# Forgetting attention: in the first and third pair of query blocks, both blocks' last keys in one PSUM bank with one causal mask of 256 columns

## The chip, the cores and the metric

The kernel runs on one core of a Trainium2 chip. The metric is the time of one execution on the device, in microseconds (us), of the slowest core; here that is the only core. Five engines work beside each other and wait for one another through semaphores: PE (TensorE, matmuls and transposes), DVE (VectorE), ACT (ScalarE), POOL (GpSimd) and SP (SyncE, which issues the transfers). Matmul results go to PSUM, which the kernel uses as eight banks of 512 fp32 columns by 128 partitions.

## The reference, cut to what matters

The reference is a two-layer trunk over 1024 tokens of width 1024. Layer 0 mixes tokens with "forgetting attention" (16 heads of 64), layer 1 with gated linear attention; each is followed by a SwiGLU channel mixer. Only the attention is touched by the change. For every head and every block of 128 queries it computes this over the keys up to the block's end:

```python
for blk in range(S // Q_BLOCK):
    qs, qe = blk * Q_BLOCK, (blk + 1) * Q_BLOCK
    logits = jnp.einsum('bqhd,bkhd->bhqk', q[:, qs:qe], k[:, :qe]).astype(jnp.float32) * scale
    logits = logits + cum[:, :, qs:qe, None] - cum[:, :, None, :qe]
    mask = (qs + jnp.arange(Q_BLOCK))[:, None] >= jnp.arange(qe)[None, :]
    logits = jnp.where(mask[None, None], logits, -jnp.inf)
    p = jax.nn.softmax(logits, axis=-1).astype(v.dtype)
    outs.append(jnp.einsum('bhqk,bkhd->bqhd', p, v[:, :qe]))
```

The causal mask only bites in the last 128 keys of a block, where the queries stand against themselves.

## The kernel before, in words

**Units.** The eight blocks of 128 queries are taken in four pairs, g = 0 to 3; pair g holds the blocks 2g and 2g+1, whose keys are (2g+1)·128 and (2g+2)·128 wide. Heads go in pairs too: p = 0 to 7, a = 0 or 1. So there are 8·2·4 = 64 units (p, a, g), and within one head the pairs of blocks are taken in the order 0, 3, 1, 2 (ORDER, L1342). "First pair" below is g = 0 (128 and 256 keys), "third pair" is g = 2 (640 and 768 keys). There are 16 units of each.

**Scores (scores, L1259 to L1292).** For each of the two blocks (qi) the keys are cut into pieces of at most 512 columns (L1274). A piece gets a PSUM bank from the ring sr, which has two banks (L831). PE writes the piece with two matmuls, one with K1 (L1279) and one with KL, the low-order part of the keys (L1280). Both run 128 query columns as stationary operand, so each is preceded by a load of weights. The last piece of a block ends with a third matmul: the identity times a constant mask of 128 columns, both bf16, adds 1e30 above the diagonal (L1282). The scores are held with the sign turned, so a softmax subtracts the minimum. DVE then adds the cumulated forget gates to the piece, writes it to the SBUF tile lp and takes the running minimum along the row (L1285, two records each: the pass itself and the reading of its accumulator). When both pieces of a block are through, ACT takes the exponential with that minimum as bias and sums the row (L1289, again two records), DVE takes the reciprocal (L1290) and POOL scales the row (L1291).

**Outputs (outputs, L1294).** PE transposes the scaled rows in 128x128 blocks (trans, L1311), up to four to a bank of the ring tr (three banks); ACT and DVE split each into a high and a low part (L174, L175); then PE multiplies with the values (pv, L1323 and L1325). Outputs of a unit are emitted after the scores of the next unit (attention, L1354), so a third pair is transposed after the scores of the next head's first pair.

**The order.** Scores and outputs are generators; each yield gives a cost. weave (L130, called at L1386) takes turns between the attention of head pair p and the projections of head pair p+1 (matmuls of 512 and 256 columns, L305 to L307), in proportion to the costs yielded against the two totals 23.0 and 31.0. The attention of a p yields more than the 23.0 it is weighed by, so the projections run out first and the last part of every p has none beside it. A planner then orders each engine's instructions with an estimate of every duration; the order is fixed when the kernel is built, and LAGS (L1343) keeps a projection from running more than 18 attention steps ahead on PE. After the last p, the output projection and the channel mixer follow (from L1452).

Of the kernel before, what the change touches and what calls it, by code (L numbers as in the profile page):

```python
# [9 lines left out]
F32 = mybir.dt.float32  # L10
# [3 lines left out]
AF = mybir.ActivationFunctionType  # L14
ALU = mybir.AluOpType

P = 128
# [3 lines left out]
HALF = 512  # L21
# [32 lines left out]
def trunk(ctx, tc, x, c, ada_w, ada_b, norm1_g, norm2_g, ffn_w_in, ffn_w_out,  # L54
          fox_w_in, fox_b_f, fox_w_out, gla_w_in, gla_w_a2, gla_b_a, gla_g_o,
          gla_w_out, final_g, out, dbg=None, stop=None):
    nc = tc.nc
# [9 lines left out]
    def ps_rings(*counts):  # L67
        r, i = [], 0
        for n in counts:
            r.append(Ring(psp, [f"b{j}" for j in range(i, i + n)]))  # L70
            i += n
        assert i <= 8
        return r
# [35 lines left out]
    def psl(t, n=1):  # L109
        return slice(t * P, (t + n) * P)  # L110
# [49 lines left out]
    identb = cst.tile([P, P], BF16, name="identb")  # L160
# [9 lines left out]
    maskb = cst.tile([P, P], BF16, name="maskb")  # L170
# [265 lines left out]
    def last_of(e):  # L436
        return next(i for i in reversed(nc.cur_bb.bb.instructions) if i.engine == ENG[e])
# [393 lines left out]
    sr, tr, orr, pj = ps_rings(2, 3, 1, 2)  # L831
# [427 lines left out]
    def scores(u):  # L1259

        p, a, g = u
        t = qkt[p]
        Qs, K1, KL = (t["QA"], t["KA"], t["KLA"]) if a == 0 else (t["QB"], t["KB"], t["KLB"])
        cm = cums[2 * p + a]
        if g < 2:
            both = lpr([P, (4 * g + 3) * P], F32, f"lp{p}{a}{g}")
            lps = [both[:, 0:(2 * g + 1) * P], both[:, (2 * g + 1) * P:]]
        else:
            lps = [lpr([P, (2 * g + 1 + i) * P], F32, f"lp{p}{a}{g}{i}") for i in range(2)]
        st = sm.tile([P, 2, 4], F32, tag="st", bufs=4, name=f"st{p}{a}{g}")  # L1270
        for qi in range(2):
            qb = 2 * g + qi
            qs, lp, Wd, mcur = psl(qb), lps[qi], (qb + 1) * P, 3e38
            cuts = (0, 384, 640) if Wd == 640 else (0, Wd) if Wd <= HALF else (0, HALF, Wd)  # L1274
            for n_, (k0, k1) in enumerate(zip(cuts, cuts[1:])):
                ps = sr([P, k1 - k0], F32, f"s{p}{a}{qb}{k0}")
                early = u == (0, 0, 0)
                diag = k1 == Wd
                nc.tensor.matmul(ps, Qs[:, qs], K1[:, k0:k1], start=True, stop=False)  # L1279
                nc.tensor.matmul(ps, Qs[:, qs], KL[:, k0:k1], start=False, stop=not diag)  # L1280
                if diag:
                    nc.tensor.matmul(ps[:, k1 - k0 - P:], identb, maskb, start=False, stop=True)  # L1282
                mnew = st[:, qi, n_:n_ + 1]
                with tc.issue_after(v_last) if early else ExitStack():
                    nc.vector.tensor_tensor_reduce(lp[:, k0:k1], ps, cm[:, k0:k1], 1.0, mcur,  # L1285
                                                   ALU.add, ALU.min, mnew)
                mcur = mnew
                yield max(0.22, 0.00085 * (k1 - k0))
            nc.scalar.activation(lp, lp, AF.Exp, bias=mcur, scale=-1.0, accum_out=st[:, qi, 2:3])  # L1289
            nc.vector.reciprocal(st[:, qi, 3:4], st[:, qi, 2:3])  # L1290
            nc.gpsimd.tensor_scalar(lp, lp, st[:, qi, 3:4], 1.0, op0=ALU.mult, op1=ALU.mult)  # L1291
        return lps  # L1292

    def outputs(u, lps):  # L1294
# [59 lines left out]
    def attention(p):  # L1354
        for a in range(2):
            for g in ORDER:
                u = (p, a, g)
                lps = yield from scores(u)
                if p:
                    ada0p(0.8)  # L1360
                if pending[0] is not None:
                    yield from finish(*pending[0])
                pending[0] = (u, lps)
        if p == 7:
            yield from finish(*pending[0])
# [15 lines left out]
    v_last = last_of("D")  # L1381
# [95 lines left out]
    early = [s_ for s_ in rest if s_ in list(vring.q) + qk_all + list(cumr.q)]  # L1477
# [1042 lines left out]
```

## Time and profile before

| what | us |
|---|---|
| median of 3 timed runs | 2358.49 |
| lowest and highest of them | 2356.21 and 2358.67 |
| the profiled execution's own time | 2358.25 |
| its span, first to last instruction | 2356.5 |
| attention on PE, first to last start of its matmuls | 95.3 to 601.8 |

The profile is of one execution. Its span leaves out 1.75 us around the instructions (2358.25 - 2356.5). Records give the start of an instruction and how long it took; of matmuls, which are pipelined, the distance from one start to the next is the better measure of what one costs.

### The profile page before, as it was taken

Reading aid. Unit: us, or ns where it says so; the run is one execution under the profiler, and the core shown is the slowest. Engines: PE = TensorE matmul, PEld = TensorE weight load, DVE = VectorE, ACT = ScalarE, POOL = GpSimd, SP = SyncE. Lnnn points to the kernel's source line nnn. Section 1 sums busy time; section 2 is a strip of 40 time slices with the busy share of each in tenths; the row PEclk is TensorE's granted clock in tenths of the full one; section 3 lists DMA queues with packets and bytes.
Section 4 is the critical chain, followed back from the end, with each engine's and each line's share of the span. In section 5 each row is a group of like instructions: output and inputs, shape, how many; then the busy total and the mean of one; then the engine's idle time right before and its main releaser. Section 6 shows DMA issues by size and latency. Waiting matters only on the chain. (4 is left out here: it accounts for less than half of the span.)

```text
span 2356.5 us, 35548 instructions
## 1 busy us (share of the span) xinstructions
PE 2327.9 (99%) x12168; PEld 1980.9 (84%) x12168; DVE 1778.1 (75%) x2957; ACT 1122.5 (48%) x2166; POOL 1126.3 (48%) x995
## 2 busy tenths in 40 slices
PE   8999999999999999999999999999999999999999
PEld 7888888888888888888878898898888888888878
DVE  6578787886788888886787665678787777876776
ACT  6656655665443333345234644344453333345235
POOL 1334544533445666664643431345446665665631
PEclk8999999999999999999999999999999999999999
DMA  8423333332435545458674442554435444458574
GB/s 266 144 90 106 102 121 95 121 129 96 143 101 167 187 161 173 160 192 298 224 272 158 138 134 87 146 182 166 145 111 164 165 150 155 148 204 298 199 277 136
DMA packets 349614, 383.38 MB, mean 163 GB/s; under 512 B 25372, under 2 KB 286648, under 8 KB 349432
## 3 DMA queue, kind: packets, MB, share of 16 engines
q1 hardware_dynamic: 349432, 381.11, 49.1%
q8 instruction: 96, 1.57, 0.3%
q14 instruction: 86, 0.70, 0.1%
HBM read 279.76 MB, written 101.25 MB: 162 GB/s over the span
## 5 line engine op out<-in xcount | busy, mean ns | idle before, releaser
L174 ACT CAST o_s<-xv_s 128x512 fp32r<-128x512 f32 (+1 forms) x392 | 236.5, 610 | 343.0 <-PE p_b L307 250.0
L175 DVE TENSOR_TENSOR o_s<-xv_s,o_s 128x512 fp32r<-128x512 f32 (+1 forms) x392 | 331.9, 851 | 44.8 <-ACT o_s L174 44.0
L307 PE MATMUL p_b<-B,o_s 128*128 128x512 f32 x608 | 236.0, 389 | 0.0
L306 PE MATMUL p_b<-B,o_s 128*128 128x512 f32 x608 | 235.9, 389 | 0.0
L305 PE MATMUL p_b<-B,o_s 128*128 128x512 f32 x608 | 235.4, 390 | 0.0
L938 POOL TENSOR_TENSOR ex_s<-xv_s,xv_s 128x512 f32<-128x512 f32 (+1 forms) x64 | 96.2, 1503 | 259.0 <-DMA xv_s<-in_ffn_w_in_dram 119.9
L1291 POOL TENSOR_SCALAR lp_s<-lp_s,st 128x128 f32<-128x128 f32 (+7 forms) x128 | 98.0, 769 | 246.3 <-DVE st L1290 231.1
L305 PE MATMUL p_b<-T,o_s 128*128 128x512 f32 x480 | 186.8, 389 | 0.0
L306 PE MATMUL p_b<-T,o_s 128*128 128x512 f32 x480 | 186.7, 389 | 0.0
L307 PE MATMUL p_b<-T,o_s 128*128 128x512 f32 x480 | 181.1, 389 | 0.0
L307 PEld LDWEIGHTS p_b<-B,o_s 128*128 128x128 f32 x608 | 114.1, 188 | 23.8
L305 PEld LDWEIGHTS p_b<-B,o_s 128*128 128x128 f32 x608 | 114.2, 188 | 23.7 <-DVE x L1657 0.2
L306 PEld LDWEIGHTS p_b<-B,o_s 128*128 128x128 f32 x608 | 114.2, 188 | 23.5
L1289 ACT ACTIVATE lp_s<-lp_s,st 128x128 f32<-128x128 f32 (+7 forms) x128 | 99.3, 776 | 58.0 <-DVE st L1285 56.7
L940 POOL TENSOR_TENSOR xv_s<-ex_s,xv_s 128x512 f32<-128x512 f32 (+1 forms) x64 | 94.4, 1475 | 59.5 <-DVE o_s L175 56.5
L1657 DVE TENSOR_TENSOR ex_s<-ex_s,p_b 128x512 f32<-128x512 f32 x140 | 94.3, 682 | 37.4 <-PE p_b L307 37.3
L174 ACT CAST pt_s<-t_b 128x512 fp32r<-128x512 f32 (+1 forms) x160 | 79.7, 547 | 72.9 <-PE t_b L1311 72.3
L950 POOL TENSOR_TENSOR xv_s<-xv_s,xv_s 128x512 f32<-128x512 f32 x48 | 65.2, 1358 | 96.3 <-issue 52.3
L175 DVE TENSOR_TENSOR pt_s<-t_b,pt_s 128x512 fp32r<-128x512 f32 (+1 forms) x160 | 96.3, 630 | 15.9 <-ACT pt_s L174 15.4
L246 POOL TENSOR_TENSOR w_l_s<-w__s,w_h_s 128x256 fp32r<-128x256 f32 x90 | 69.4, 799 | 76.6 <-ACT w_h_s L242 58.8
L307 PEld LDWEIGHTS p_b<-T,o_s 128*128 128x128 f32 x480 | 90.1, 188 | 18.7
L306 PEld LDWEIGHTS p_b<-T,o_s 128*128 128x128 f32 x480 | 90.1, 188 | 18.6
(1532 smaller groups left out, 7396.8 us busy)
## 6 DMA issues: line engine op xcount, KB each, us to landing
xv_s<-in_ffn_w_in_dram SPq DMA_DIRECT2D x176, 256.0 KB, 3.2
hid_B<-x SPq DMA_DIRECT2D x66, 512.0 KB, 2.8
ad_s<-in_ada_w_dram SPq DMA_DIRECT2D x384, 64.0 KB, 2.3
hid_T<-x SPq DMA_DIRECT2D x44, 512.0 KB, 2.9
xv_s<-in_ffn_w_out_dram SPq DMA_DIRECT2D x88, 256.0 KB, 3.2
ada_s<-in_ada_w_dram SPq DMA_DIRECT2D x96, 128.0 KB, 2.8
T2o<-hid_T SPq DMA_DIRECT2D x22, 512.0 KB, 7.6
T1o<-hid_T SPq DMA_DIRECT2D x22, 512.0 KB, 8.6
```

Source lines behind the costliest of these rows:

```text
L174: nc.scalar.copy(hi, src)
L175: nc.vector.tensor_sub(lo, src, hi.bitcast(F32))
L246: (nc.gpsimd if i < 3 else nc.vector).tensor_sub(lo[:, cs], rw[:, cs], hi[:, cs].bitcast(F32))
L305: nc.tensor.matmul(ps, ah, bh, start=start, stop=False, skip_group_check=chain)
L306: nc.tensor.matmul(ps, ah, bl, start=False, stop=False, skip_group_check=chain)
L307: nc.tensor.matmul(ps, al, bh, start=False, stop=stop, skip_group_check=chain)
L938: nc.gpsimd.tensor_add(s1, a21, a22)
L940: nc.gpsimd.tensor_sub(a11, s1, a11)
L950: nc.gpsimd.tensor_sub(r[A12], r[A12], r[A11])
L1289: nc.scalar.activation(lp, lp, AF.Exp, bias=mcur, scale=-1.0, accum_out=st[:, qi, 2:3])
L1291: nc.gpsimd.tensor_scalar(lp, lp, st[:, qi, 3:4], 1.0, op0=ALU.mult, op1=ALU.mult)
L1657: nc.vector.tensor_add(d, d if src is None else dest(G, src), ps)
```

## The change

In the first and the third pair (g = 0 and g = 2) the last 128 or 256 keys of the two blocks are put side by side into one bank. For g = 0 that is 128 columns of the first block and 256 of the second; for g = 2 it is 256 of each, after a piece of 384 and one of 512 columns in banks of their own. PE writes all four score matmuls of the shared bank, then one matmul of the identity with the mask read twice (256 columns), which lands on the last 128 columns of each block. Only the first matmul of the bank carries the start flag. Then DVE takes the two parts, and each block's exponential, reciprocal and scaling follow its own part. The widths of the DVE passes, the exponentials and the scalings are the same as before. The number of pieces per bank, the places of the yields and the yielded cost of the first pair (0.22 in place of twice 0.22) are not. The second and the fourth pair (g = 1 and g = 3) keep their cuts and a mask for each block.

```diff
-            cuts = (0, 384, 640) if Wd == 640 else (0, Wd) if Wd <= HALF else (0, HALF, Wd)
-            for n_, (k0, k1) in enumerate(zip(cuts, cuts[1:])):
-                ps = sr([P, k1 - k0], F32, f"s{p}{a}{qb}{k0}")
...
+        least = [[], []]
+
+        def pair(o_, qi, k0, k1, start, stop):
+            qs = psl(2 * g + qi)
+            nc.tensor.matmul(o_, Qs[:, qs], K1[:, k0:k1], start=start, stop=False, skip_group_check=not stop)
+            nc.tensor.matmul(o_, Qs[:, qs], KL[:, k0:k1], start=False, stop=stop, skip_group_check=not stop)
+
+        def low(o_, qi, k0, k1):
+            got = least[qi]
+            mnew = st[:, qi, len(got):len(got) + 1]
+            with tc.issue_after(v_last) if u == (0, 0, 0) else ExitStack():
+                nc.vector.tensor_tensor_reduce(lps[qi][:, k0:k1], o_, cm[:, k0:k1], 1.0, got[-1] if got else 3e38,
+                                               ALU.add, ALU.min, mnew)
+            got.append(mnew)
+
+        def exps(qi):
+            lp = lps[qi]
+            nc.scalar.activation(lp, lp, AF.Exp, bias=least[qi][-1], scale=-1.0, accum_out=st[:, qi, 2:3])
             nc.vector.reciprocal(st[:, qi, 3:4], st[:, qi, 2:3])
             nc.gpsimd.tensor_scalar(lp, lp, st[:, qi, 3:4], 1.0, op0=ALU.mult, op1=ALU.mult)
+
+        W_ = [(2 * g + 1 + qi) * P for qi in range(2)]
+        if g in (0, 2):
+            cut = [0, 0] if g == 0 else [384, HALF]
+            for qi in range(2):
+                if g:
+                    ps = sr([P, cut[qi]], F32, f"s{p}{a}{g}{qi}")
+                    pair(ps, qi, 0, cut[qi], True, True)
+                    low(ps, qi, 0, cut[qi])
+                    yield 0.00085 * cut[qi]
+            n0 = W_[0] - cut[0]
+            ps = sr([P, n0 + 256], F32, f"s{p}{a}{g}")
+            pair(ps[:, 0:n0], 0, cut[0], W_[0], True, False)
+            pair(ps[:, n0:n0 + 256], 1, cut[1], W_[1], False, False)
+            m_ = ps.rearrange("p (a b) -> p a b", b=P)[:, n0 // P - 1::2]
+            nc.tensor.matmul(m_, identb, maskb.unsqueeze(1).to_broadcast([P, 2, P]), start=False, stop=True,
+                             skip_group_check=True)
+            for qi, c0, c1 in ((0, 0, n0), (1, n0, n0 + 256)):
+                low(ps[:, c0:c1], qi, cut[qi], W_[qi])
+                exps(qi)
+            yield 0.22 if g == 0 else 0.44
+            return lps
```

More of the change, by code (lines that the diff above doesn't have):

```diff
@@ L1270, in scores @@
         st = sm.tile([P, 2, 4], F32, tag="st", bufs=4, name=f"st{p}{a}{g}")
-        for qi in range(2):
-            qb = 2 * g + qi
-            qs, lp, Wd, mcur = psl(qb), lps[qi], (qb + 1) * P, 3e38
-            cuts = (0, 384, 640) if Wd == 640 else (0, Wd) if Wd <= HALF else (0, HALF, Wd)
-            for n_, (k0, k1) in enumerate(zip(cuts, cuts[1:])):
-                ps = sr([P, k1 - k0], F32, f"s{p}{a}{qb}{k0}")
[L1277 to L1289, printed above, removed]
@@ new lines, in scores @@
+        for qi in range(2):
+            cuts = (0, W_[qi]) if W_[qi] <= HALF else (0, HALF, W_[qi])
+            for k0, k1 in zip(cuts, cuts[1:]):
+                ps = sr([P, k1 - k0], F32, f"s{p}{a}{g}{qi}{k0}")
+                diag = k1 == W_[qi]
+                pair(ps, qi, k0, k1, True, not diag)
+                if diag:
+                    nc.tensor.matmul(ps[:, k1 - k0 - P:], identb, maskb, start=False, stop=True,
+                                     skip_group_check=True)
+                low(ps, qi, k0, k1)
+                yield max(0.22, 0.00085 * (k1 - k0))
+            exps(qi)
```

## The prediction, made before the changed kernel was run

> **What bounds the kernel now.** I read the page first (span, busy times, slices), then the stretch of the attention alone, then its waits on PE, then the order of time at a few places.
>
> ```profile
> span 2356.5 us, 35548 instructions
> PE 2327.9 (99%) x12168; PEld 1980.9 (84%) x12168; DVE 1778.1 (75%) x2957; ACT 1122.5 (48%) x2166; POOL 1126.3 (48%) x995
> PEclk8999999999999999999999999999999999999999
> ...
> 95.00:602.00 507.00, 501.52 (x3216) 439.15 (x3216) 378.69 (x960) 303.35 (x646) 221.36 (x316) 1.00 0.33 105
> ```
>
> PE has a record open for 99% of the span at a clock that is granted in full after the first slice. The last row is the attention by itself (us: length, busy PE, PEld, DVE, ACT, POOL; then clock and DMA): PE is open for 501.52 of 507.00 us, DVE for 378.69. PE therefore sets the pace here. From 602 us on, the page's slices show PE at 9 tenths to the end, so I let a microsecond of PE saved in the attention move everything behind it by a microsecond. The page's chain of work that ended last doesn't help: it covers 30% of the span and begins behind the attention.
>
> The waits on PE between 90 and 600 us (us in total, times, longest) are small:
>
> ```profile
> PE t_b L1311 <- POOL lp_s L1291: 2.8, 3, 1.9
> PE qk_b L305 <- DVE QB L860: 1.1, 2, 0.5
> PE s_b L1279 <- DVE st L1285: 0.4, 2, 0.3
> ```
>
> Transposes waiting for POOL's scaled rows are the largest; the wait for a score bank, which the change touches, is 0.4 us.
>
> **The change part by part.** *The masks.* A matmul's record is longer than what it costs, so I take start-to-start distances. In the order of time on PE (start, length, engine, line):
>
> ```profile
> 304.01 0.28 PE L1280 MATMUL s_b<-KLA,QA 128*128 128x256 f32 x1
> 304.14 0.23 PE L1282 MATMUL s_b<-maskb,identb 128*128 128x128 bf16 x1
> 304.18 0.36 PE L307 MATMUL vps_b<-wv_4h_s,h0l 128*128 128x256 f32 x1
> 304.38 0.28 PE L305 MATMUL vps_b<-wv_0h_s,h0h 128*128 128x256 f32 x1
> 304.49 0.28 PE L306 MATMUL vps_b<-wv_0l_s,h0h 128*128 128x256 f32 x1
> 304.61 0.28 PE L307 MATMUL vps_b<-wv_0h_s,h0l 128*128 128x256 f32 x1
> ...
> 349.17 0.28 PE L1280 MATMUL s_b<-KLA,QA 128*128 128x256 f32 x1
> 349.30 0.23 PE L1282 MATMUL s_b<-maskb,identb 128*128 128x128 bf16 x1
> 349.33 0.47 PE L305 MATMUL qk_b<-h0h,w_h_s 128*128 128x512 f32 x1
> 349.65 0.39 PE L306 MATMUL qk_b<-h0l,w_h_s 128*128 128x512 f32 x1
> 349.88 0.40 PE L307 MATMUL qk_b<-h0h,w_l_s 128*128 128x512 f32 x1
> ```
>
> A 256-column matmul in a steady row takes 0.12 us (304.49 to 304.61), a 512-column one 0.23 (349.65 to 349.88). Around the first mask, from L1280's start to the start after the next matmul, 304.38 - 304.01 = 0.37; two 256-column steps would be 0.24, so the mask costs 0.13. Around the second, 349.65 - 349.17 = 0.48 against 0.12 + 0.23 = 0.35: 0.13 again. The mask's own step is only 0.04; the rest is that the matmul behind it is stretched from 0.12 to 0.20, or from 0.23 to 0.32.
>
> ```profile
> L1282 PE MATMUL s_b<-maskb,identb x128: 229/230/233, 95.5 to 586.8; 128*128 128x128 bf16 x128
> ```
>
> There are 128 masks (8 blocks by 16 heads). The change turns two into one in 32 units (16 heads, two pairs each), so 96 stay, 32 of them 256 wide. What does a mask of 256 columns cost? The trace shows none. From below: a 256-column matmul with a weight load of its own steps at 0.12, so it may cost no more than the 128-column mask did. From above: 256 more columns cost 0.23 - 0.12 = 0.11, so 128 more could add 0.055. The stretch of the matmul behind the mask speaks for the low end: it says that the 128 columns are too short to cover the next weight load, so 128 more fill time that is lost today. I take 0.13 for it, as for a narrow one. Saved: 32 x 0.13 = **4.2 us**; with the upper price 32 x (0.13 - 0.055) = 2.4, with 0.12 for the wide mask 4.5.
>
> A rule of the Trainium skill speaks against this. "TensorE: Matmul & The Clock Gate", section "Back-to-back issue gap", gives an isolated matmul its columns over 2.4 GHz plus 2.5 ns; by that, one mask of 256 columns saves 2.5 ns against two of 128, and 32 of them 0.1 us. The same section says that this undercounts small matmuls where each has a weight load, and the 0.13 us above agrees with that.
>
> *What stays.* Score matmuls, DVE passes, exponentials and scalings keep their number and widths; no transfer is added, and SP's queue has nothing moved past it. One weight load per removed mask goes too; it is inside the 0.13.
>
> *The bank.* Four pieces of a third pair become three, two of a first pair one, so a shared bank is held until two DVE passes are through. The ring has two banks and the next score piece behind a shared bank takes the other one. PE's waits for a score bank are 0.4 us in all; between nothing and twice that, I take no change.
>
> *The later exponential.* This is the cost. In the third pair the first block's last part now stands in the shared bank, behind the 512-column piece of the second block and ahead of its last part. At the end of one p, on DVE (L1285), ACT (L1289) and POOL (L1291):
>
> ```profile
> 344.02 0.48 DVE L1285 CUSTOM_DVE_ANT_0 lp_s<-s_b,cum_s,st 128x256 f32<-128x256 f32 x1
> 344.61 0.83 ACT L1289 ACTIVATE lp_s<-lp_s,st 128x640 f32<-128x640 f32 x1 [0.55 <-DVE st L1285]
> 345.34 0.19 ACT L1289 ACTIVATION_READ_ACCUMULATOR lp_s<-lp_s,st 128x1 f32 x1
> 348.04 0.48 DVE L1285 CUSTOM_DVE_ANT_0 lp_s<-s_b,cum_s,st 128x256 f32<-128x256 f32 x1
> 348.45 0.08 DVE L1285 DVE_READ_ACCUMULATOR2_ANT st<- 128x1 f32 x1
> 348.93 0.94 ACT L1289 ACTIVATE lp_s<-lp_s,st 128x768 f32<-128x768 f32 x1
> 351.49 0.91 POOL L1291 TENSOR_SCALAR lp_s<-lp_s,st 128x768 f32<-128x768 f32 x1 [4.79 <-DVE st L1290]
> ```
>
> Before, the first block's minimum (344.02) and exponential (344.61) are done some 4 us ahead of the second's. After, the two minima are taken one behind the other: 0.48 + 0.08 = 0.56 us in front of the second's on DVE, and the first's exponential, 0.83 + 0.19 = 1.02, directly in front of the second's on ACT. It begins 0.56 before the second minimum is there, so the second exponential starts 1.02 - 0.56 = 0.46 after it. In all the second block's scaled rows come 0.56 + 0.46 = **1.0 us later**, the first block's some 4 us.
>
> Who waits for that? Behind a waiting transpose stands all of PE's queue. In the middle of a p there is room, at its end there is none:
>
> ```profile
> 316.30 0.91 POOL L1291 TENSOR_SCALAR lp_s<-lp_s,st 128x768 f32<-128x768 f32 x1 [0.46 <-DVE st L1290]
> 320.87 1.03 PE L1311 MATMUL t_b<-ident,lp_s 128*128 128x128 f32 x8
> ...
> 352.23 0.23 PE L1282 MATMUL s_b<-maskb,identb 128*128 128x128 bf16 x1
> 352.45 1.09 PE L1311 MATMUL t_b<-ident,lp_s 128*128 128x128 f32 x8
> 353.30 0.48 PE L305 MATMUL qk_b<-h0h,w_h_s 128*128 128x512 f32 x1
> ```
>
> In the first case POOL ends at 317.21 and PE transposes at 320.87, 3.7 us later. In the second it ends at 351.49 + 0.91 = 352.40 and PE starts at 352.45; the mask before stepped 0.22 rather than 0.04, so PE stood for some 0.2. Behind those transposes lie projections (353.30) that the planner can put ahead of them: it knows of the later exponential and fills with steps of 0.23, so what is left is about half such a step, 0.12, at the seven ends with a next p, less where POOL is early: I take 0.12 at six, **0.7 us**. Without that cover it is the first rival.
>
> *The sum.* 2358.25 (the profiled execution) - 4.2 + 0.7 = 2354.75, that is 3.5 less. The median of the runs is 2358.49, 0.24 above the profiled one; 3.5 below it is **2355.0 us**.
>
> **The rivals.** *A, slower: the late third pair stalls PE.* The planner's order holds a transpose at the ends of a p that the real exponential doesn't meet. Seen today once in full:
>
> ```profile
> 410.88 0.95 POOL L1291 TENSOR_SCALAR lp_s<-lp_s,st 128x640 f32<-128x640 f32 x1 [8.95 <-DVE st L1290]
> 411.88 0.55 PE L1311 MATMUL t_b<-ident,lp_s 128*128 128x128 f32 x3 [1.88 <-POOL lp_s L1291]
> ```
>
> PE stood 1.88 us there for the first block's rows. The price is 1.0 to 1.6 us an end (1.6 where the whole first exponential stands in front, 0.56 + 1.02), seven ends: 7 to 11, and 3 to 7 after the 4.2: middle 2358.49 + 4.8 = 2363.3. It cancels the gain from 0.6 an end (4.2 / 7). For it: no cover at the ends. Against it: work to put there, and only 2.8 us of such waits today. "Perfetto Trace Analysis", section "Matmuls", of the Trainium skill points the same way, asking that independent groups rotate through banks so that emptying one overlaps the next; the 0.4 us above is all that the trace shows of such a wait.
>
> *B, a smaller gain: the wide mask pays for its columns.* Saved 2.4 rather than 4.2, less 0.7: 2356.8. By the page's isolated rule it would be 2358.49 - 0.1 + 0.7 = 2359.1.
>
> *C, a larger gain: the new order also loses today's waits.* The 1.88 above, the rest of the 2.8 and the 0.4 go: 4.2 + 2.8 + 0.4 = 7.4, so 2351.1. The lower cost yielded for the first pair leaves projections beside 0.44 more of each p's attention (two heads by 0.22), which speaks for it; that the exponentials come later speaks against.
>
> *D, nothing is saved:* the planner puts other work between the shared bank's matmuls so that masks and loads cost the same sum: 2358.5.
>
> **How the numbers follow.** My forecast (2355.0, by itself 2353.3 to 2357.0) 0.48; A 0.12; B 0.13; C 0.25; D 0.02. This kernel's measurement can tell about 0.2%, 4.7 us, from no change: faster means below 2353.8, slower above 2363.2. Faster: C's 0.25 and 0.08 of the forecast, 0.33. Slower: half of A and what lies beyond it, 0.08. Within: 0.59. For 8 in 10 the range takes in the forecast, B, most of C and the lower half of A: 2350.0 to 2361.5.
>
> **What would show it.** Right: 96 masks in place of 128, 32 of them 256 wide; the matmul behind a wide mask no longer stretched; the same counts of DVE, ACT and POOL instructions; PE's busy time in the attention some 4 us less; PE's waits for POOL's scaled rows below 4 us. Wrong in B's way: behind a wide mask's start the next step is 0.1 rather than 0.04 and the one after still stretched. Wrong in A's way: PE's idle time before L1311 at the ends of a p near 1 us each. Any change behind 602 us that isn't a plain shift would be outside this account.

## The result: 0.6% slower

| | us |
|---|---|
| before, median of 6 runs | 2359.19 (2356.21 to 2360.67) |
| after, median of 6 runs | 2372.65 (2371.73 to 2375.54) |
| ratio, with its 95% interval | 1.0061 [1.0048, 1.0074] |
| the profiled execution after, its span | 2375.54, 2373.8 |

That is 13.5 us more, where 3.5 less was forecast and 2361.5 was the top of the range. The profiled execution is the slowest of the six after, 2.9 us above their median. The page of the kernel after, its span and its busy times:

```profile
span 2373.8 us, 35478 instructions
...
PE 2336.1 (98%) x12136; PEld 1986.5 (84%) x12136; DVE 1792.2 (75%) x2957; ACT 1120.9 (47%) x2166; POOL 1130.6 (48%) x995
```

PE has 32 matmuls fewer (12168 - 12136), the other engines have the counts of before. The view of the score bank's tile by line (count, then least, median and largest duration in ns) shows which:

```profile
L1320 PE MATMUL s_b<-maskb,identb x64: 229/230/233, 104.6 to 593.2; 128*128 128x128 bf16 x64
L1306 PE MATMUL s_b<-maskb,identb x32: 283/283/284, 98.2 to 604.0; 128*128 128x256 bf16 x32
```

96 masks in place of 128, 32 of them 256 wide. The change did what it says, and the time still went up. Where? Stretches of the kernel after (us: length, busy PE, PEld, DVE, ACT, POOL; then clock, DMA share, GB/s):

```profile
95.00:602.00 507.00, 489.75 (x3106) 426.45 (x3105) 381.36 (x945) 296.10 (x633) 220.44 (x312) 0.99 0.33 104
294.00:298.00 4.00, 1.98 (x8) 1.47 (x9) 3.35 (x15) 2.98 (x9) 1.11 (x2) 0.86 0.84 245
298.00:302.00 4.00, 4.00 (x24) 3.79 (x23) 1.61 (x4) 1.82 (x4) 1.37 (x3) 0.72 0.02 9
60.00:70.00 10.00, 10.00 (x43) 8.49 (x43) 4.72 (x9) 5.44 (x9) 2.74 (x3) 0.66 1.06 379
```

The first row answers to the one that the prediction began with: in the same 507 us from 95 to 602 PE now has a record open for 489.75 instead of 501.52 us, so it stands for 12 us that it did not stand before. The rest of the span splits by the first and last start of the attention's matmuls on PE. Before the attention there are 2.4 us more (97.7 against 95.3); the change touches nothing there, and the last row shows a granted clock of 0.66 in that stretch. The run e6 below, whose engines run the very order of before, has the same 0.66 there and starts its attention at 97.7 too, so I leave these 2.4 us out. In the attention there are 14.5 more (521.0 against 506.5). Behind it, to the end, 1755.1 against 1754.7: a plain shift.

PE's waits between 90 and 640 us of the kernel after (us in total, times, longest):

```profile
PE o_b L1358 <- DVE oT_s L1373: 5.5, 4, 1.6
PE s_b L1275 <- DVE st L1282: 5.0, 6, 1.8
PE t_b L1344 <- POOL lp_s L1290: 1.4, 4, 0.5
```

The wait on which the forecast spent its argument, for POOL's scaled rows, fell from 2.8 to 1.4. Two others came. The score bank was 0.4 and is 5.0. The first row is new: value products wait for the one output bank (the ring orr has one) until DVE has added its content to oT. Before, the view has no such row.

The end of one head pair shows how. On PE, in the order of time (start, length, what it did; in brackets how long PE stood and for whom), after:

```profile
290.76 0.28 PE L1358 MATMUL o_b<-pt_s,v_s 128*128 128x256 f32 x1
290.88 0.37 PE L1275 MATMUL s_b<-KB,QB 128*128 128x256 f32 x1
...
291.45 0.28 PE L1306 MATMUL s_b<-maskb,identb 128*128 128x256 bf16 x1
291.49 0.32 PE L1275 MATMUL s_b<-KA,QA 128*128 128x128 f32 x1
...
292.04 0.28 PE L1306 MATMUL s_b<-maskb,identb 128*128 128x256 bf16 x1
292.08 0.48 PE L305 MATMUL qk_b<-h0h,w_h_s 128*128 128x512 f32 x1
292.40 0.39 PE L306 MATMUL qk_b<-h0l,w_h_s 128*128 128x512 f32 x1
292.63 0.39 PE L307 MATMUL qk_b<-h0h,w_l_s 128*128 128x512 f32 x1
...
292.98 0.34 PE L1356 MATMUL o_b<-pt_s,v_s 128*128 128x128 f32 x2
294.70 0.47 PE L1275 MATMUL s_b<-KA,QA 128*128 128x512 f32 x1 [1.38 <-DVE st L1282]
...
297.22 1.65 PE L1358 MATMUL o_b<-pt_s,v_s 128*128 128x256 f32 x6 [1.32 <-DVE oT_s L1373]
```

And on DVE, in the same stretch:

```profile
289.33 1.00 DVE L505 SCALAR_TENSOR_TENSOR acc_s<-ada_s,c,acc_s 128x256 f32<-128x256 f32 x2 [2.75 <-DMA ada_s<-in_ada_w_dram]
...
292.60 1.15 DVE L175 TENSOR_TENSOR pt_s<-t_b,pt_s 128x512 fp32r<-128x512 f32 x2
293.66 0.48 DVE L1282 CUSTOM_DVE_ANT_0 lp_s<-s_b,cum_s,st 128x256 f32<-128x256 f32 x1
...
294.67 0.42 DVE L1282 CUSTOM_DVE_ANT_0 lp_s<-s_b,cum_s 128x256 f32<-128x256 f32 x1
...
295.14 0.68 DVE L858 SCALAR_TENSOR_TENSOR QA<-qk_b,QA 64x512 fp32r<-64x512 f32 x1
295.83 0.69 DVE L860 SCALAR_TENSOR_TENSOR QB<-qk_b,QB 64x512 fp32r<-64x512 f32 x1
...
296.75 0.42 DVE L1373 TENSOR_TENSOR oT_s<-o_b,ot 64x256 f32<-64x256 f32 x1
```

PE fills the third pair's shared bank (290.88 to 291.49) and directly behind it the next head pair's first shared bank (291.49 to 292.08), in 1.2 us. DVE is still splitting transposes until 293.66; then it has four minima in a row. The next piece on PE, for the fourth pair (294.70), can only have the third pair's bank, and waits 1.38 us for its minima. The value products end at 292.98 + 0.34 = 293.32, but the add that empties their bank stands in DVE's row behind the four minima and two evacuations of projections (L858, L860), and starts at 296.75, 3.4 us later; PE stands another 1.32. Before, at the same place, DVE:

```profile
286.08 0.68 DVE L1285 CUSTOM_DVE_ANT_0 lp_s<-s_b,cum_s 128x512 f32<-128x512 f32 x1
...
286.80 0.42 DVE L1340 TENSOR_TENSOR oT_s<-o_b,ot 64x256 f32<-64x256 f32 x1
287.25 0.48 DVE L1285 CUSTOM_DVE_ANT_0 lp_s<-s_b,cum_s,st 128x256 f32<-128x256 f32 x1
...
287.66 0.29 DVE L1285 CUSTOM_DVE_ANT_0 lp_s<-s_b,cum_s 128x128 f32<-128x128 f32 x1
...
289.67 0.42 DVE L1285 CUSTOM_DVE_ANT_0 lp_s<-s_b,cum_s 128x256 f32<-128x256 f32 x1
```

There the pieces come one by one, and the add slips in ahead of the last minimum of the third pair.

The first of the DVE rows of after shows something else: DVE came late to this end, since until 289.33 it had stood 2.75 us for a transfer of modulation weights (ada_w), which it multiplies and adds up beside the attention. It stood 2.63 us in the same way ahead of the end at 420 us. These are the two dearest ends: 2.70 and 3.42 of the 10.5 us of the two waits. Between 90 and 640 us before has even more of such waits (14.3 us, after 10.5), but ahead of its ends only one within 4 us is over 1 us long (1.4). They aren't the whole of it: at the end at 357 us PE stands 1.23 for the add with no such wait ahead.

To compare kernels I go through all steps from one start of PE's matmuls to the next in the attention. The usual length of a step is the median for the same shape in that kernel; where a step is more than 0.15 us longer, the excess is counted as a stall. The seven ends are the 8 us on each side of the first score matmul of a next head pair:

| kernel | attention, us | stalls at the ends | stalls elsewhere | clock at half rate |
|---|---|---|---|---|
| before | 506.5 | 6.8 | 2.1 | 0 |
| after | 521.0 | 14.7 | 8.7 | 6.8 |

The 14.5 us more are then 7.9 at the ends and 6.6 elsewhere, less 4.2 for the masks, and a part of 6.8 us at half rate, which costs 3.4 at most and is partly counted in the stalls: 10.3 to 13.7 against the 14.5.

### The profile page after: what moved, and what is told of

The parts are those of the page before. It is cut to its first block, busy times and chain, and to the rows that moved or that the text cites. A ratio compares the mean times of both kernels' runs of the same rounds, so it can differ in the third digit from the quotient of the medians.

```text
span 2373.8 us, 35478 instructions
## 1 busy us (share of the span) xinstructions
PE 2336.1 (98%) x12136; PEld 1986.5 (84%) x12136; DVE 1792.2 (75%) x2957; ACT 1120.9 (47%) x2166; POOL 1130.6 (48%) x995
## 5 line engine op out<-in xcount | busy, mean ns | idle before, releaser
L175 DVE TENSOR_TENSOR pt_s<-t_b,pt_s 128x512 fp32r<-128x512 f32 (+1 forms) x160 | 95.6, 630 | 13.8 <-ACT pt_s L174 13.5
```

Source lines behind the costliest of these rows:

```text
L175: nc.vector.tensor_sub(lo, src, hi.bitcast(F32))
```

## The experiments

Four explanations were tried. **The order at the seam:** with two shared banks and the lower cost yielded for the first pair (0.22 in place of twice 0.22), the weave puts fewer projections beside the next head pair's first scores, and the two banks' minima stand in a heap. **The late exponential:** rival A of the prediction. **One bank:** one of the two shared banks alone does it. **The output bank:** there is only one. (The expectations number their own theories: 1 is the late exponential of the third pair, 2 a shared bank held too long, 3 the lower cost.) All runs, each with the median of the kernel before on the same chip:

| run | median, us | before | ratio [95%] |
|---|---|---|---|
| e1_first_only | 2366.58 | 2361.22 | 1.0023 [1.0006, 1.0041] |
| e2_third_only | 2359.62 | 2361.22 | 0.9991 [0.9982, 1.0001] |
| e3_two_masks | 2374.90 | 2361.22 | 1.0069 [1.0052, 1.0085] |
| e4_old_cost | 2362.10 | 2361.22 | 1.0008 [0.9997, 1.0018] |
| e5_shared_first | 2359.71 | 2361.89 | 0.9992 [0.9981, 1.0002] |
| e6_late_exp | 2362.84 | 2361.89 | 1.0009 [1.0000, 1.0019] |
| e7_low_cost | 2363.48 | 2361.89 | 1.0004 [0.9994, 1.0013] |
| e8_first_old_cost | 2363.51 | 2361.89 | 1.0006 [0.9996, 1.0015] |
| e9_two_out_banks | 2379.29 | 2361.20 | 1.0075 [1.0057, 1.0093] |
| e10_before_two_out | 2384.53 | 2361.20 | 1.0094 [1.0079, 1.0109] |
| e11_cost_033 | 2370.66 | 2361.20 | 1.0047 [1.0027, 1.0067] |
| e12_first_low | 2369.24 | 2361.20 | 1.0034 [1.0021, 1.0046] |
| e13_weight | 2375.21 | 2360.13 | 1.0056 [1.0039, 1.0074] |
| e14_cost_066 | 2359.06 | 2360.13 | 0.9996 [0.9983, 1.0008] |
| e15_best | 2360.36 | 2360.13 | 0.9998 [0.9989, 1.0006] |

### One shared bank at a time, two masks, the old cost

The first pair alone shares a bank, the third keeps its four pieces (against after):

```diff
-        if g in (0, 2):
+        if g == 0:
...
-            cuts = (0, W_[qi]) if W_[qi] <= HALF else (0, HALF, W_[qi])
+            cuts = (0, 384, 640) if W_[qi] == 640 else (0, W_[qi]) if W_[qi] <= HALF else (0, HALF, W_[qi])
```

> Only the first pair shares a bank and a mask; the third pair keeps its four pieces and two masks as before. Theory 1 (the third pair's late last parts and exponentials crowd DVE and ACT at the ends of a head pair): the cost is the third pair's, so this run is near the kernel before, less 16 masks of 0.13 us: 2354 to 2361 us. Theory 2 (a shared bank is held too long, in either pair): half of the loss, 2364 to 2368. Theory 3 (the first pair's halved cost in the interleaving upsets the order): most of the loss stays, 2368 to 2374.

The third pair alone (against after):

```diff
-        if g in (0, 2):
+        if g == 2:
```

> Only the third pair shares a bank and a mask; the first pair keeps two pieces, two masks and two yields of 0.22. Theory 1: most of the loss stays, 2367 to 2374 us. Theory 2: half of it, 2364 to 2368. Theory 3: the loss is gone, 2354 to 2361.

Both pairs shared, but with a mask of 128 columns for each block (against after):

```diff
-            m_ = ps.rearrange("p (a b) -> p a b", b=P)[:, n0 // P - 1::2]
-            nc.tensor.matmul(m_, identb, maskb.unsqueeze(1).to_broadcast([P, 2, P]), start=False, stop=True,
-                             skip_group_check=True)
+            for c1 in (n0, n0 + 256):
+                nc.tensor.matmul(ps[:, c1 - P:c1], identb, maskb, start=False, stop=c1 > n0,
+                                 skip_group_check=True)
```

> As the changed kernel, but the shared bank ends with two masks of 128 columns, one behind the other, in place of one of 256. It measures what a merged mask saves. At 0.13 us each, 32 of them: 4.2 us slower than the changed kernel, some 2377 us; if the wide mask pays for its columns, 2.4 us slower, some 2375; if it saves nothing, the same 2372.6.

After, with the cost yielded for the first pair as before:

```diff
-            yield 0.22 if g == 0 else 0.44
+            yield 0.44
```

> As the changed kernel, but the first pair yields 0.44 as it did before in all, so that the projections are interleaved at the old pace. Theory 3: back to 2354 to 2360 us. Theories 1 and 2: no change from 2372.6 beyond 2 us either way.

Measured: the first pair alone costs 5.4 us, the third alone takes 1.6 off, with an interval that reaches no change, and both together cost 13.5; so some 10 of the 13.5 belong to neither alone. The third alone also settles the late exponential. In its trace the first block's exponential starts 0.95 us ahead of the second's (median of 16), where before it starts 4.76 ahead: it is as late as in after, and the run is no slower. Two masks in place of one stand 2.3 us above after by the medians (2374.90 - 2372.65), but 0.2 if each is taken against its own before (13.7 and 13.5): the masks aren't the loss, and what one is worth can't be told from this run. And one number does nearly all: with 0.44 in place of 0.22 the time falls by 10.5 us by the medians; against its own before it is 0.9 above, where after is 13.5 above. The same end of a head pair in e4, on DVE:

```profile
288.98 0.48 DVE L1282 CUSTOM_DVE_ANT_0 lp_s<-s_b,cum_s,st 128x256 f32<-128x256 f32 x1
...
290.47 0.42 DVE L1282 CUSTOM_DVE_ANT_0 lp_s<-s_b,cum_s 128x256 f32<-128x256 f32 x1
...
291.00 0.42 DVE L1373 TENSOR_TENSOR oT_s<-o_b,ot 64x256 f32<-64x256 f32 x1
...
293.06 0.68 DVE L858 SCALAR_TENSOR_TENSOR QA<-qk_b,QA 64x512 fp32r<-64x512 f32 x1 [1.05 <-ACT QB L857]
```

and on PE:

```profile
288.66 0.28 PE L1306 MATMUL s_b<-maskb,identb 128*128 128x256 bf16 x1
288.70 0.48 PE L306 MATMUL qk_b<-h0l,w_h_s 128*128 128x512 f32 x1
...
289.86 0.48 PE L307 MATMUL qk_b<-h0h,w_l_s 128*128 128x512 f32 x1
...
290.64 0.40 PE L307 MATMUL qk_b<-h0h,w_l_s 128*128 128x512 f32 x1
...
291.73 0.96 PE L1358 MATMUL o_b<-pt_s,v_s 128*128 128x256 f32 x6
```

The shared banks and the four minima are the same. But PE has a projection between the two banks' scores (288.70) and four behind the second (289.86 to 290.87), so DVE is through with the minima at 290.9 and adds at 291.00; the evacuation comes behind the add. The value products start at 291.73 with no wait. DVE also has no wait for a transfer ahead of this end. In the whole attention of e4 the wait for the add is 2.4 us and that for the score bank 3.4, where after has 5.5 and 5.0; the stalls at the ends are 8.2 (after 14.7), elsewhere 4.3 (8.7).

### The cost alone, the lateness alone, the first pair with the old cost, another order

Before, with half the cost for the first pair:

```diff
-                yield max(0.22, 0.00085 * (k1 - k0))
+                yield max(0.11 if g == 0 else 0.22, 0.00085 * (k1 - k0) * (g > 0))
```

> The kernel before with one thing changed: the first pair yields 0.11 twice in place of 0.22 twice. Banks, masks and order within a unit are the old ones. Theory 3a (the pace alone is the cause): 2366 to 2372 us. Theory 3b (the pace hurts only together with the shared banks): within 3 us of the kernel before.

Before, with the first block's exponential, reciprocal and scaling of a third pair written in the program behind the second block's last minimum, meant as the lateness of rival A alone:

```diff
+            held.append((lp, mcur, qi))
+            if g == 2 and qi == 0:
+                continue
+            for lp, mcur, q_ in held:
+                nc.scalar.activation(lp, lp, AF.Exp, bias=mcur, scale=-1.0, accum_out=st[:, q_, 2:3])
...
+            held.clear()
```

> The kernel before with one thing changed: in the third pair the first block's exponential, reciprocal and scaling are issued after the second block's last minimum, with banks, masks and yields as before. It is the lateness of rival A by itself. If lateness costs 1.0 to 1.6 us at each of seven ends of a head pair: 2366 to 2372. If the planner covers it, as the run with the third pair alone suggests: within 3 us of the kernel before.

e1 with the old cost:

```diff
-            yield 0.22 if g == 0 else 0.44
+            yield 0.44
```

> As the run with the first pair alone, but it yields 0.44. Theory 3 (pace): some 2 us faster than the kernel before, 2357 to 2361 where that is at 2360, and 5 us or more faster than the run with 0.22. If the first pair's shared bank itself costs, it stays at 5 us above the kernel before.

Both shared, the old cost, and in the third pair the shared bank written first, the pieces of 384 and 512 behind it (against after):

```diff
-                exps(qi)
-            yield 0.22 if g == 0 else 0.44
+                if g == 0:
+                    exps(qi)
+            yield 0.44
+            for qi in range(2):
+                if g:
+                    ps = sr([P, cut[qi]], F32, f"s{p}{a}{g}{qi}")
+                    pair(ps, qi, 0, cut[qi], True, True)
+                    low(ps, qi, 0, cut[qi])
+                    yield 0.00085 * cut[qi]
+                    exps(qi)
```

> Both pairs share banks and masks and yield the old sums (0.44 and 1.20), but in the third pair the shared bank is written first and the pieces of 384 and 512 columns after it, so that the first block's exponential can start before the second's piece of 512. If what is left in the run with the old cost (4.2 us of masks saved and about as much lost again) is the late exponential, this one is 3 to 4 us faster than that run, 3 to 4 us faster than the kernel before. If the saved masks are the smaller thing or the order doesn't matter, it is the same as that run.

e6 did not test the lateness. On ACT, at the end that the prediction shows:

```profile
347.00 0.83 ACT L1294 ACTIVATE lp_s<-lp_s,st 128x640 f32<-128x640 f32 x1 [0.55 <-DVE st L1286]
...
351.33 0.94 ACT L1294 ACTIVATE lp_s<-lp_s,st 128x768 f32<-128x768 f32 x1
```

The two exponentials start 4.33 us apart, as before (344.61 and 348.93). The planner put the first one back where it was: PE, DVE, ACT and POOL all run the same operations on the same tiles and shapes in the same order as in the kernel before. So e6's 0.9 us is what two builds of one order can differ by here. That the late exponential isn't the cause rests on e2 above.

The lower cost alone (e7), with a bank for each block, costs 1.6 us, within its interval of nothing; both shared banks with the old cost (e4) cost 0.9. So it takes the low cost *and* the shared banks. For the first pair alone that is less clear: 1.6 with the old cost, where 2 less than before was expected, and 5.4 with the low one, with intervals that overlap. PE's waits in e7 tell the two apart:

```profile
PE s_b L1279 <- DVE st L1285: 4.9, 5, 1.5
...
PE o_b L1325 <- DVE oT_s L1340: 0.4, 2, 0.2
```

The wait for the score bank comes with the low cost alone, without any shared bank, as long as in after (5.0). The wait for the add does not: it is 0.4 here, 2.4 in e4, and 5.5 only where both meet. The stalls of e7 are 9.1 at the ends and 2.2 elsewhere, of e6, with the order of before, 7.5 and 2.1.

With the shared bank first and the old cost (e5) the kernel is 2.2 us below before, where 3 to 4 were expected, with an interval that reaches no change. In its profiled run the attention takes 506.6 us, the 506.5 of before: stalls of 8.4 and 3.0, together 2.5 more than before, eat most of what the masks give.

### The output bank, and the cost in doses

After with two output banks, one taken from the transposes; and before with the same, as its control:

```diff
-    sr, tr, orr, pj = ps_rings(2, 3, 1, 2)
+    sr, tr, orr, pj = ps_rings(2, 2, 2, 2)
```

> The changed kernel with one PSUM bank moved from the transposes (three to two) to the outputs (one to two), so that the next unit's value products needn't wait until DVE has added the last ones up. In the profile of the changed kernel PE waits 5.5 us for that add at the ends of head pairs. If that wait is a cause: 4 to 8 us faster than the changed kernel's 2372.6 (with the half-rate clock windows that follow such waits), against its own control. If the waits are only a symptom of a late DVE, they move to the next thing: the same time within 2 us.

> Control: the kernel before with the same two banks for transposes and two for outputs. It tells what the move of a bank does by itself. Expected: 0 to 5 us slower than the kernel before, since three transposed tiles of a third pair no longer fit.

After with 0.33, and e5 with 0.22:

```diff
-            yield 0.22 if g == 0 else 0.44
+            yield 0.33 if g == 0 else 0.44
```

> The changed kernel, but the first pair yields 0.33, half way between 0.22 (2372.6 us) and 0.44 (2362.1). If the yielded cost acts through how much projection work lies at the ends of head pairs, the time lies between: 2364 to 2370. If the planner's order merely falls well or badly, it can lie anywhere from 2358 to 2375, outside that stretch as well as within.

```diff
-            yield 0.44
+            yield 0.22 if g == 0 else 0.44
```

> Shared bank first in the third pair, as in the run that was a little faster than the kernel before, but the first pair yields 0.22 as in the change. If the yielded cost is the cause by whatever order in the third pair: 2366 to 2372. If it takes the late last parts of the third pair as well: 2358 to 2362.

PE's largest wait in e9:

```profile
PE t_b L1344 <- DVE pt_s L175: 6.3, 10, 1.5
```

and in its control e10:

```profile
PE t_b L1311 <- DVE pt_s L175: 6.9, 13, 1.7
```

With two banks for the outputs no wait for the add is left, and the changed kernel is 5.2 us *below* its control (2379.29 against 2384.53, four runs each, with intervals that overlap), where with one output bank it was 13.5 above. The loss is gone; the gain can't be told from noise. But two transpose banks cost 23 us by themselves, where 0 to 5 were expected, and the order is another one throughout, so this supports the output bank as the cause without proving it: that the change is slower hangs on how the banks are shared out.

The doses go one way in after's order: 0.22 gives 1.0061, 0.33 1.0047, 0.44 1.0008; the intervals of the first two overlap, and 0.33 came out 0.7 us above the stretch expected. In e5's order 0.22 gives 1.0034 and 0.44 0.9992. PE's waits in e12, the same order as e5 with 0.22:

```profile
PE o_b L1360 <- DVE oT_s L1375: 5.4, 4, 1.7
PE s_b L1275 <- DVE st L1282: 2.7, 5, 1.2
```

The wait for the add is that of after (5.5) again, while e5 has 2.6. This order loses less than after's, 8.0 us.

### Pace or place, and the best of them

The lower cost does two things: it lets fewer projections run beside the whole attention of a head pair, and it lets fewer run at one place, behind the first pair. After with another weight for the weave gets the average pace back and leaves the place:

```diff
-        weave(attention(p), 23.0, chain(*parts), 31.0 if p < 6 else 20.8, LAGS)
+        weave(attention(p), 22.6, chain(*parts), 31.0 if p < 6 else 20.8, LAGS)
```

> The changed kernel with the attention of a head pair weighed by 22.6 in place of 23.0, which restores the average pace of projections per attention step that the lower cost of the first pair took away, but not their share right behind a first pair. If the average pace is the cause: 2358 to 2364 us, as with the old cost. If it is the place, few projections between the next head pair's first unit and the second pair's value products: 2367 to 2374, no gain on the changed kernel.

e5 with more than the old cost for the first pair, and e5 once more in five rounds:

```diff
-            yield 0.44
+            yield 0.66 if g == 0 else 0.44
```

> Shared bank first in the third pair, the first pair yields 0.66 (0.22 gave 2369.2, 0.44 gave 2359.7). If more projections behind the first pair keep covering the ends of head pairs: 2353 to 2358. If 0.44 was enough, or the added share is missing elsewhere: 2359 to 2364.

> The run with the shared bank first and the old cost once more, in five rounds, for its interval against the kernel before: 0.9992 so far, with both saved masks (4.2 us, 0.18%) and what is lost at the ends in it. Expected 0.998 to 1.000.

The other weight gains nothing (1.0056; the wait for the add is 5.3 us, that for the score bank 6.2). So it isn't the average pace, and the place is what is left. More than 0.44 gives nothing further, and e5, measured again, is 0.2 us off before: 0.9998 [0.9989, 1.0006]. No version beats the kernel before by more than can be told.

## Why the prediction was wrong

**What bounds the kernel: right.** PE sets the pace, and a microsecond lost in the attention moves the end by one; behind it is a plain shift (1755.1 us against 1754.7).

**The masks: right in price, the reason wrong.** 32 are gone. A wide mask steps 0.04 us (292.04 to 292.08) and the matmul behind it 0.32 (292.08 to 292.40) where the next takes 0.23: what a narrow one costs, so 0.13 for it was right, though its record is 53 ns longer. Over all masks of after, wide and narrow ones alike cost a median of 0.12 us ahead of 256 or 512 columns and 0.07 ahead of 128, so the 4.2 us is at the high end. The reason given was wrong: the matmul behind a wide mask is stretched as before. As a saving in time the 4.2 us stays unmeasured; 0.2 to 2.3 from e3 and 5.2 from e9 and e10 are all within the noise. PE's busy time in the attention, forecast some 4 us less, is 2.7 more (503.75 against 501.02), with the stretches at half rate in it.

**The bank: the step that failed.** The forecast took "no change" from a wait of 0.4 us and bounded it by "nothing to twice that". A wait of today says nothing of one that the change makes: the pieces behind a shared bank can only have the other bank, and the two shared banks follow each other at the end of each head pair. In after PE stands 5.0 us for the score bank, and 5.5 for the add that empties the one output bank, which stands behind the same heap of minima. That second bank was not in the forecast at all, and it is the wait that only the change as a whole has: the score bank's is 4.9 in e7 without a shared bank. The forecast gave all that is slower than 2363.2 a chance of 0.08.

**The yielded cost: its sign was wrong.** It stood only under rival C, as what "leaves projections beside 0.44 more of each p's attention, which speaks for it". It is the term that decides, together with the shared banks: 10.5 us between 0.22 and 0.44 with them, 1.6 without. That the end of a head pair has projections to fill with was counted on in the next step ("the planner can put ahead of them"); the same edit took them from there.

**The later exponential: small, as taken.** 0.7 us were taken. No run has the lateness alone, since e6 does not have it; e2 has it with 16 masks fewer and is 1.6 us below before, and PE's wait for scaled rows went down from 2.8 to 1.4. Whether it is 0.7 or nothing can't be told.

**Rival A: right place, wrong wait.** The ends of a head pair are where most of it is lost, 7.9 us over seven, 1.1 an end, by luck in the band of 1.0 to 1.6 that A gave. But PE stands there for the output and the score bank, not for the third pair's rows, and the time was past A's own 2363.3.

**Shown, and not.** Shown by runs: that the low cost together with the shared banks makes the loss (e4, e7), that neither the late exponential (e2) nor the average pace (e13) does, and, by rows, which waits it becomes. Argued from rows alone: that the planner leaves PE's two banks side by side because the weave gives it fewer projections there. Open: how much of the 7.9 us at the ends comes from DVE's waits for the modulation weights, which in after fall right ahead of the two dearest ends; and how much of the 6.6 us elsewhere comes from DVE being held by POOL, below. Nothing was run that changes either alone.

## What to carry to other kernels

A cost that a generator yields to an interleaving is a part of the change: keep its sum when steps are merged, and measure it apart. Where a planner orders the instructions, look in the trace whether an experiment has the order that it was written for, before its time is read. Where two pieces come to share a bank, look at the seam between units, and ask for each ring with one or two banks what the engine that frees it has in its row ahead of the freeing instruction. A small wait in the profile of before says what there is to gain by removing it, never what is lost when something longer is put there.

## What the runs showed of the hardware

**The clock falls in the middle of a kernel that is 98% busy.** At the end shown above PE stood 1.38 and 1.32 us within 4 us, and the granted clock is 0.86 and then 0.72 of full in the two stretches 294 to 298 and 298 to 302: at half rate that is 2 · 4 · (0.14 + 0.28) = 3.4 us. The six value products at 297.22 take (298.67 - 297.22) / 6 = 0.24 us each where a 256-column matmul takes 0.12. In all, 6.8 us of after's attention are at half rate, none of before's. That isn't fixed by the order: e6, with the order of before, has a clock of 0.57 from 415 to 419 us, which is 3.4 us at half rate, right after the same wait of 1.9 us for POOL that before has without such a stretch. The Trainium skill, "TensorE: Matmul & The Clock Gate", section "What's actually happening", gives half rate after an idle window of some 3.4 us and full rate after a busy one of that length. The 3.4 us to come back agree; for the fall, no single wait on PE in after's attention was longer than 1.8.

**DVE held by POOL.** At four places of after's attention a subtraction of weights on DVE that mostly takes 0.4 to 1.0 us took 4.3 to 5.4. The kernel after, DVE:

```profile
194.33 5.41 DVE L246 TENSOR_TENSOR wv_0l_s<-wv_s,wv_0h_s 128x256 fp32r<-128x256 f32 x1 [0.35 <-ACT wv_0h_s L242]
199.66 0.41 DVE L1373 TENSOR_TENSOR oT_s<-o_b,ot 64x256 f32<-64x256 f32 x1
```

and POOL:

```profile
193.88 1.42 POOL L246 TENSOR_TENSOR w_l_s<-w__s,w_h_s 128x256 fp32r<-128x256 f32 x2
195.26 0.73 POOL L468 TENSOR_TENSOR acc_s<-acc_s 128x256 f32<-128x256 f32 x1
195.95 0.73 POOL L246 TENSOR_TENSOR w_l_s<-w__s,w_h_s 128x256 fp32r<-128x256 f32 x1
196.64 2.12 POOL L246 TENSOR_TENSOR wv_0l_s<-wv_s,wv_0h_s 128x256 fp32r<-128x256 f32 x3
198.72 0.73 POOL L468 TENSOR_TENSOR acc_s<-acc_s 128x256 f32<-128x256 f32 x1
```

POOL runs without a break from 193.88 to 199.45, and DVE's record ends at 199.74. The add and a minimum stand behind it. Two such records are of 5.4 and two of 4.3 us; in before the longest is 2.3, in e4 there is one of 5.4, and e5 has none above 1.1. The Trainium skill, "SBUF — State Buffer", section "Who interferes with whom", says that a DVE instruction with two SBUF inputs contends with a GpSimd instruction that reads SBUF, and calls the port pair that they share an exclusive lock. The rows agree, and suggest that a whole row of POOL instructions can pass before DVE gets its turn; that it is the port which holds DVE is read from the times alone.
